# Input forms of a block-product MLP: odd tiles used where they lie, the residual's loads moved, fewer steps of a task queue

## The chip, the core and the metric

The kernel runs on one core of one Trainium2 chip. The metric is the device time of one execution in microseconds (us). Inputs and output lie in device memory (HBM); five engines work in parallel on tiles in the on-chip memory: PE multiplies matrices, DVE, ACT and POOL compute on vectors, and SP, ACT and POOL issue DMA transfers.

## The reference, cut to what matters

The reference is one decoder block in float32 for 512 tokens, D = 2048 and a hidden width of 8192. Attention, a gated recurrence and their projections come first and are not touched. The change lies in the MLP at the end:

```python
h2 = rms_norm(x, norm2_w[l]) * (1.0 + scale2) + shift2
ff = jnp.square(jax.nn.relu(h2.astype(dt) @ w_ff1[l])) @ w_ff2[l]
x = x + (gate2 * ff.astype(jnp.float32)).astype(dt)
```

`h2` is the normalised input of the title, `x` in the last line the residual.

## The kernel before, in words

**Numbers.** Every float32 operand of PE is split into a high part (a cast, on ACT) and a low part (the value minus the high part, on DVE), and each product is three matmuls: high by high, high by low, low by high. So `whi`, `vhi` are high parts of weights, `wlo`, `vlo` low ones, and a pair `hi`, `lo` of 128x512 tiles is one 128-channel slice of `h2`, transposed, for all 512 tokens. There are 16 such channel tiles, even and odd ones; all stay on chip in the pool `hp`.

**Plain stage.** The first four of the 16 hidden groups of 512 columns are computed directly (`hidden`, `first_hidden`; matmuls at L205 to L207, weight casts at L39, subtractions at L40). Meanwhile a queue of small tasks (`tasks`; one `tick()` advances it by one `yield`) prepares the **input forms**: `input_forms(u)`, u = 0 to 3, copies four channel tiles into `fs` (L1047, ACT) and `make_forms` turns them into seven block combinations by four subtractions or additions (L1017 to L1020), splits each into high and low (L1025, L1026) through staging tiles `part`, and stores them to HBM (L1028, issued by POOL): `h_hid`, `h_lod`. The same helper stores the forms of the hidden activations, `f_hid` and `f_lod`.

**Block products.** The other six pairs of hidden groups, and the whole second matrix, are computed as 2x2 block matrices with seven products instead of eight, numbered 1 to 7 and run in `order`. The first matrix has six blocks of 1024 columns; the second has two halves of the columns, q = 0 and 1, with four steps c = 0 to 3 each, which add up. One `product` consists of four steps u, and each step needs 12 matmuls (L1157 to L1159) with one `vhi` (cast at L1143) and one `vlo` (L1144). Some products first combine raw weight tiles (L1127, DVE). There is one tile each of `vhi` and `vlo` for each u: the cast for step u of the next product can start when PE is done with step u of the present one. Four raw weight tiles stand in each of four pools; SP loads the next one (L1119, 512 KB) when the last user of the old one is done. POOL loads the operands: four loads of 512 KB for a product, `Fh` and `Fl` (L1095), into four buffers each, two products ahead. Products 4 and 2 of the first matrix use the tiles `R` instead, four loads of 1 MB, loaded once and kept in the pool `res`.

**Around it.** After the first product 5 of a block, and of q = 0, c = 0, `turned` transposes the finished hidden columns and starts their forms. `residual_in(q)` issues nine loads on ACT's own queue, `gate` (L1270) and eight tiles `d` of the residual (L1274, 256 KB each); they are needed at c = 3. It is called at the end of c = 0 and placed behind the last copy `a` (L1318). The tile framework's scheduler sets the order of the instructions of each engine.

**Semaphores of transfers.** Transfers of SP and ACT together take eight completion semaphores in turn, called DMAHW0 to DMAHW7 in the listings below; those of POOL take DMASW0 to DMASW7. An issue waits until the transfer that had its semaphore before has landed. An engine issues in order, so an issue that waits on ACT holds up the casts behind it.

Of the kernel before, what the change touches and what calls it, by code (L numbers as in the profile page):

```python
# [8 lines left out]
F32 = mybir.dt.float32  # L9
# [35 lines left out]
def hybrid_block(ctx, tc, x, c, positions, norm1_w, w_ada, b_ada, w_in, q_norm_w, k_norm_w,  # L45
# [176 lines left out]
    ph = ctx.enter_context(ExitStack())  # L222
# [7 lines left out]

    def pair(i):

        return [hp.tile([P, S], F32R, name=f"{c}{i}", tag=f"{c}{i}") for c in ("hi", "lo")]
# [5 lines left out]
    for i in range(NK):  # L239
        pair(i)  # L240
    hhi, hlo, spare = [], [], []

# [762 lines left out]
    PLAIN = 4  # L1005
    KG = 4

    def forms_in_dram(name, n):
        return [dr.tile([n * FORMS * P, 512], F32, name=f"{name}_{c}d").rearrange("(g i p) n -> g i p n", i=FORMS, p=P)
                for c in ("hi", "lo")]  # L1010

    fparts, hparts = forms_in_dram("f", NG), forms_in_dram("h", KG)

    def make_forms(fs, dst, g, stage, in_place=False):

        a21, a11, a22, a12, s1, s2, s4 = (fs[:, i] for i in range(FORMS))
        dve.tensor_tensor(s1, a21, a22, op=ALU.add)  # L1017
        dve.tensor_tensor(a21, a11, a21, op=ALU.subtract)
        dve.tensor_tensor(s2, s1, a11, op=ALU.subtract)
        dve.tensor_tensor(s4, a12, s2, op=ALU.subtract)  # L1020
        yield
        for a, b in ((0, 2), (2, 4), (4, 6), (6, 7)):
            hi = stage()[:, 0:b - a]
            lo = fs[:, a:b].bitcast(F32R) if in_place else stage()[:, 0:b - a]
            act.copy(hi, fs[:, a:b])  # L1025
            dve.tensor_tensor(lo, fs[:, a:b], hi.bitcast(F32), op=ALU.subtract)  # L1026
            for d, t in zip(dst, (hi, lo)):
                pool.dma_start(d[g, a:b].rearrange("i p n -> p i n"), t.rearrange("p i a t -> p i (a t)").bitcast(F32))  # L1028
            yield

    def block(fs, j):
# [7 lines left out]
        return stg.tile([P, FORMS, 2, 256], F32, name="fs", bufs=1)  # L1039

    def plain_stage():
        return stg.tile([P, 2, 2, 256], F32R, name="part", bufs=7)

    def input_forms(u):
        fs = plain_forms()
        for j in range(4):
            act.copy(block(fs, j), halves(uT[4 * u + j]))  # L1047
# [19 lines left out]

    st_.close()
    pw.close()
    ph.close()  # L1070

    s_ = {}
    pools = {}
    for n, b in (("raw12", 4), ("spl3", 1), ("s15", 1), ("raw22", 4), ("spl1", 1), ("spl2", 1), ("s67", 1), ("raw21", 4),
                 ("fs2", 1), ("stA", 3), ("raw11", 4), ("spl0", 1), ("stB", 1), ("fp", 4)):
        pools[n] = ctx.enter_context(tc.tile_pool(name=n, bufs=b, reuse_waits="tile"))
        if n[0:2] in ("s1", "s6"):
            for i in n[1:3]:
# [12 lines left out]
    def operand(src, c, i):

        def load(t, d, g):
            n = t.shape[1]
            pool.dma_start(t.rearrange("p g a t -> p g (a t)").bitcast(F32),  # L1095
                           d[g:g + n, slot_of[i]].rearrange("g p n -> p g n"))
# [12 lines left out]

    def weights(view, g0, c0, order):  # L1110
# [8 lines left out]
                    nc.sync.dma_start(raw, view[:, g0 + u, e, :, c0 + n * 512:c0 + (n + 1) * 512])  # L1119
# [9 lines left out]
    def part(i, u, w, first):  # L1129

        b11, b12, b21, b22 = (w[u, e, n] for e in range(2) for n in range(2))
        if i == 5:
            sum_of(b11, b12, b11, first)
        if i == 6:
            sum_of(b11, b22, b11, first)
        if i == 7:
            sum_of(b12, b22, b12, first)
        if i == 4:
            sum_of(b11, b11, b21, first)
        src = {1: b11, 5: b11, 6: b11, 4: b11, 7: b12, 2: b21, 3: b22}[i]  # L1140
        hi = pools[f"spl{u}"].tile([P, 2, 512], F32R, name="vhi")
        lo = pools[f"spl{u}"].tile([P, 2, 512], F32R, name="vlo")
        act.copy(hi, src)  # L1143
        split_done.append(dve.tensor_tensor(lo, src, hi.bitcast(F32), op=ALU.subtract))  # L1144
        return hi, lo

    def product(i, src, c, w, tag, by_tile, first, early):

        banks = [bank("f2", tag=tag) for _ in range(2)]
        fh, fl = operand(src, c, i)  # L1150

        def mm(u, whi, wlo, ts_):
            for a in range(2):
                for t in ts_:
                    ts = slice(t * P, (t + 1) * P)
                    first, end = u + a == 0, u + a == KG
                    pe.matmul(banks[t], lhsT=fh[u][:, a, ts], rhs=whi[:, a], start=first, stop=False)  # L1157
                    pe.matmul(banks[t], lhsT=fh[u][:, a, ts], rhs=wlo[:, a], start=False, stop=False)  # L1158
                    pe.matmul(banks[t], lhsT=fl[u][:, a, ts], rhs=whi[:, a], start=False, stop=end)  # L1159
# [167 lines left out]

# [50 lines left out]
```

## Time and profile before

| | before |
|---|---|
| time, median of 3 runs (lowest to highest) | 2330.82 us (2326.27 to 2336.61) |
| the profiled execution: its time / its span | 2319.27 us / 2317.5 us |
| PE busy in the span | 2234.7 us (96%) |
| DVE / ACT / POOL busy | 1826.0 / 1094.9 / 457.6 us |
| mean granted PE clock | 0.991 |
| bytes moved | 606.71 MB |

The span is the time from the first to the last instruction of the profiled execution. "Busy" of an engine is the sum of its instructions' times; PE's matmuls overlap, so a busy PE can still stand at half its clock. The plain stage with its input forms runs from about 1060 to 1200 us of the span, the first matrix's block products until about 1700, the second matrix to the end: q = 0 starts c = 1 at about 1780 and c = 2 at about 1855, q = 1 at about 2085 and 2160.

### The profile page before, as it was taken

The numbers are of one execution on the slowest core, as the hardware profiler recorded it, in microseconds if no ns is written. First come the engines' busy times: TensorE is split into PE (matmuls) and PEld (weight loads), VectorE is DVE, ScalarE is ACT, GpSimd is POOL, SyncE is SP. The second block draws the span as 40 slices with busy tenths as digits, with TensorE's granted clock in tenths as the row PEclk, the third lists the DMA queues.
The fourth block names the chain that finished last, engine by engine and source line by source line (L and its number), as shares of the span: only waits on it lengthen the run. The fifth ranks groups of instructions, "written<-read, shape, count | busy, mean of one in ns | idle before, by whom it ended". The sixth has DMA issues, their size and how long they took to land.

```text
span 2317.5 us, 33148 instructions
## 1 busy us (share of the span) xinstructions
PE 2234.7 (96%) x11769; PEld 1830.5 (79%) x11769; DVE 1826.0 (79%) x2773; ACT 1094.9 (47%) x1942; POOL 457.6 (20%) x668
## 2 busy tenths in 40 slices
PE   4899999999999998999999999999998999999999
PEld 3787877887778877878887888888886888888887
DVE  6999777677876574679768988988895788967878
ACT  5555434443444552447644656555563333343332
POOL 1000022000230000001342323323232222222221
PEclk9999999999999999999999999999999999999999
DMA  9798455556554256745999799889889987999884
GB/s 327 248 339 309 130 168 159 184 168 206 173 169 159 73 188 203 231 159 181 367 379 392 253 344 355 298 301 379 312 294 365 331 281 269 362 339 330 284 300 164
DMA packets 264695, 606.71 MB, mean 262 GB/s; under 512 B 23284, under 2 KB 44032, under 8 KB 264528
## 3 DMA queue, kind: packets, MB, share of 16 engines
q1 hardware_dynamic: 186800, 332.54, 42.5%
q0 software_dynamic: 72832, 262.60, 30.9%
q10 hardware_dynamic: 4896, 9.44, 1.2%
q8 instruction: 93, 1.52, 0.3%
q14 instruction: 74, 0.61, 0.1%
HBM read 522.68 MB, written 81.81 MB: 261 GB/s over the span
## 4 chain that ended last, share of the span: by engine, by line
PE 60%; DMA 14%; DVE 13%; issue 8%; ACT 2%; POOL 2%; SPq 0%; ACTq 0%; DVEq 0%; POOLq 0%
PE f L1159 10%; PE f L1158 10%; PE f L1157 10%; DMA araw<-in_w_ada_dram 7%; PE prj L197 5%; PE prj L199 4%; PE prj L198 4%; DVE acc L129 3%; PE f L207 2%; PE f L206 2%; PE f L205 2%; DMA f_lod<-fs 2%; DMA Fl<-h_lod 2%; DVE wlo L40 2%; PE prj L206 2%
## 5 line engine op out<-in xcount | busy, mean ns | idle before, releaser
L1143 ACT CAST vhi<-raw 128x1024 fp32r<-128x1024 f32 x392 | 412.8, 1055 | 548.3 <-PE f L1159 438.6
L1144 DVE TENSOR_TENSOR vlo<-raw,vhi 128x1024 fp32r<-128x1024 f32 x392 | 476.5, 1222 | 154.7 <-ACT vhi L1143 146.8
L1157 PE MATMUL f<-vhi,Fh 128*128 128x512 f32 x1376 | 538.0, 391 | 8.7 <-DMA Fh<-h_hid 3.2
L1158 PE MATMUL f<-vlo,Fh 128*128 128x512 f32 x1376 | 538.7, 391 | 3.0 <-DVE vlo L1144 3.0
L1159 PE MATMUL f<-vhi,Fl 128*128 128x512 f32 x1376 | 537.5, 391 | 1.4 <-DMA Fl<-f_lod 1.3
L39 ACT CAST whi<-wraw 128x512 fp32r<-128x512 f32 (+1 forms) x368 | 220.1, 601 | 475.4 <-PE prj L199 343.3
L197 PE MATMUL prj<-whi,hi 128*128 128x512 f32 x896 | 367.6, 410 | 8.7 <-DVE x L921 7.4
L199 PE MATMUL prj<-whi,lo 128*128 128x512 f32 x896 | 353.4, 394 | 2.5 <-DVE lo L237 2.5
L198 PE MATMUL prj<-wlo,hi 128*128 128x512 f32 x896 | 352.4, 393 | 0.0
L40 DVE TENSOR_TENSOR wlo<-wraw,whi 128x512 fp32r<-128x512 f32 (+1 forms) x368 | 244.1, 666 | 121.5 <-ACT whi L39 118.4
L129 DVE SCALAR_TENSOR_TENSOR acc<-araw,sc,acc 128x512 f32<-128x512 f32 (+1 forms) x392 | 252.9, 672 | 97.7 <-DMA araw<-in_w_ada_dram 97.0
L1157 PEld LDWEIGHTS f<-vhi,Fh 128*128 128x128 f32 x1376 | 259.4, 189 | 63.9 <-issue 6.6
L1158 PEld LDWEIGHTS f<-vlo,Fh 128*128 128x128 f32 x1376 | 259.3, 188 | 61.8 <-DVE vlo L1144 8.3
L1159 PEld LDWEIGHTS f<-vhi,Fl 128*128 128x128 f32 x1376 | 259.3, 188 | 56.1 <-DMA Fl<-f_lod 1.8
L1127 DVE TENSOR_TENSOR raw<-raw,raw 128x1024 f32<-128x1024 f32 x224 | 268.9, 1220 | 2.5 <-DMA raw<-in_w_ff_dram 2.2
L197 PEld LDWEIGHTS prj<-whi,hi 128*128 128x128 f32 x896 | 170.2, 190 | 44.5 <-DVE x L921 8.2
L199 PEld LDWEIGHTS prj<-whi,lo 128*128 128x128 f32 x896 | 169.9, 190 | 40.8 <-DVE lo L237 3.7
L198 PEld LDWEIGHTS prj<-wlo,hi 128*128 128x128 f32 x896 | 170.7, 190 | 32.6 <-DVE wlo L40 0.4
L1095 POOL DMA_DIRECT2D Fh<-f_hid x112 | 81.1, 724 | 430.5 <-PE f L1159 415.5
L205 PE MATMUL f<-hi,whi 128*128 128x512 f32 x256 | 100.2, 391 | 0.0
L207 PE MATMUL f<-hi,wlo 128*128 128x512 f32 x256 | 99.8, 390 | 0.3 <-DVE wlo L40 0.3
L206 PE MATMUL f<-lo,whi 128*128 128x512 f32 x256 | 99.6, 389 | 0.0
(305 smaller groups left out, 2941.2 us busy)
## 6 DMA issues: line engine op xcount, KB each, us to landing
raw<-in_w_ff_dram SPq DMA_DIRECT2D x224, 512.0 KB, 10.0
araw<-in_w_ada_dram SPq DMA_DIRECT2D x384, 256.0 KB, 4.2
Fh<-f_hid POOLq DMA_DIRECT2D x112, 512.0 KB, 6.5
Fl<-f_lod POOLq DMA_DIRECT2D x112, 512.0 KB, 7.7
wraw<-in_w_in_dram SPq DMA_DIRECT2D x104, 512.0 KB, 4.0
Fh<-h_hid POOLq DMA_DIRECT2D x60, 512.0 KB, 6.8
Fl<-h_lod POOLq DMA_DIRECT2D x60, 512.0 KB, 8.3
f_hid<-part POOLq DMA_DIRECT2D x48, 512.0 KB, 7.8
```

The costliest lines, as they stand in the source:

```text
L39: nc.scalar.copy(hi, src)
L40: (eng or nc.vector).tensor_tensor(lo, src, hi.bitcast(F32), op=ALU.subtract)
L129: dve.scalar_tensor_tensor(acc, raw[:, k - k0], vec[:, k:k + 1], acc, op0=ALU.mult, op1=ALU.add)
L197: pe.matmul(banks[ti], lhsT=hi[:, ts], rhs=whi, start=first, stop=False)
L198: pe.matmul(banks[ti], lhsT=hi[:, ts], rhs=wlo, start=False, stop=False)
L199: pe.matmul(banks[ti], lhsT=lo[:, ts], rhs=whi, start=False, stop=last)
L1127: dve.tensor_tensor(dst, a, b, op=ALU.subtract)
L1143: act.copy(hi, src)
L1144: split_done.append(dve.tensor_tensor(lo, src, hi.bitcast(F32), op=ALU.subtract))
L1157: pe.matmul(banks[t], lhsT=fh[u][:, a, ts], rhs=whi[:, a], start=first, stop=False)
L1158: pe.matmul(banks[t], lhsT=fh[u][:, a, ts], rhs=wlo[:, a], start=False, stop=False)
L1159: pe.matmul(banks[t], lhsT=fl[u][:, a, ts], rhs=whi[:, a], start=False, stop=end)
```

## The change

- The pool of the 16 pairs is split: even tiles in `hp0`, which is released before the block products as before, odd ones in `hp1`, which stays until the first matrix is done. The pool `res` and its four loads `R` are gone: products 4 and 2 of the first matrix take halves of the odd pairs directly.
- `input_forms` has no copies on ACT. 32 operations of 128x256 on DVE compute four combinations from the tiles into a tile `xf`; only these four are split and stored in 16 stores of 512 KB. The block a11 needs no splitting: 16 stores of 128 KB take it from the pairs. What was stored was 14 MB and is 10 MB. `xf` takes its room from the staging tiles `part`, 7 before and 5 now.
- In `product`, `tick()` stands under a condition: as before in the first matrix, but once for each product in the second. So the last hidden forms (q = 0, c = 0) advance by one step a product.
- `residual_in(q)` is called at the end of c = 1 and placed behind the last cast of that step.

```diff
-    hp = ph.enter_context(tc.tile_pool(name="hp", bufs=1, side="right"))
+    hp1 = ph1.enter_context(tc.tile_pool(name="hp1", bufs=1, side="right"))
+    hp0 = ph0.enter_context(tc.tile_pool(name="hp0", bufs=1, side="right"))
...
+    def split_out(fs, a, b, stage, in_place, dst):
+
+        hi = stage()[:, 0:b - a]
+        lo = fs[:, a:b].bitcast(F32R) if in_place else stage()[:, 0:b - a]
+        act.copy(hi, fs[:, a:b])
+        dve.tensor_tensor(lo, fs[:, a:b], hi.bitcast(F32), op=ALU.subtract)
+        for d, t in zip(dst, (hi, lo)):
+            pool.dma_start(d.rearrange("i p n -> p i n"), t.rearrange("p i a t -> p i (a t)").bitcast(F32))
...
-        return stg.tile([P, 2, 2, 256], F32R, name="part", bufs=7)
+        return stg.tile([P, 2, 2, 256], F32R, name="part", bufs=5)
 
     def input_forms(u):
-        fs = plain_forms()
-        for j in range(4):
-            act.copy(block(fs, j), halves(uT[4 * u + j]))
-        yield
-        yield from make_forms(fs, hparts, u, plain_stage)
+
+        xf = stg.tile([P, 4, 2, 256], F32, name="xf", bufs=1)
+        s1, s2, s4, s3 = (xf[:, i] for i in range(4))
+        for a in range(2):
+            ev, od = (halves(uT[4 * u + 2 * a + e]) for e in range(2))
+            a21, a11, a22, a12 = ev[:, 0], ev[:, 1], od[:, 0], od[:, 1]
+            dve.tensor_tensor(s1[:, a], a21, a22, op=ALU.add)
+            dve.tensor_tensor(s3[:, a], a11, a21, op=ALU.subtract)
+            dve.tensor_tensor(s2[:, a], s1[:, a], a11, op=ALU.subtract)
+            dve.tensor_tensor(s4[:, a], a12, s2[:, a], op=ALU.subtract)
+            for d, t in zip(hparts, h2[4 * u + 2 * a]):
+                pool.dma_start(d[u, 1, :, a * 256:(a + 1) * 256], t[:, 256:512].bitcast(F32))
+        yield
+        for a in (0, 2):
+            split_out(xf, a, a + 2, plain_stage, False, [d[u, 4 + a:6 + a] for d in hparts])
+            yield
...
-    ph.close()
+    ph0.close()
...
         if src is hparts and i in (4, 2):
-            if i not in kept:
-                kept[i] = [load(res.tile([P, KG, 2, 256], F32R, name=f"R{n}{i}"), d, 0) for d, n in zip(src, "hl")]
-            return [[t[:, u] for u in range(KG)] for t in kept[i]]
+            half = slice(256, 512) if i == 2 else slice(0, 256)
+            return [[[h2[4 * u + 2 * a + 1][j][:, half] for a in range(2)] for u in range(KG)] for j in range(2)]
...
-                tick()
+                if u == KG - 1 or src is hparts:
+                    tick()
...
-                        done = act.copy(accs7[i, t], banks[t])
+                        act.copy(accs7[i, t], banks[t])
...
-            if c == 0:
-                with tc.issue_after(done.ins):
+            if c == 1:
+                with tc.issue_after(cast_done[-1].ins):
                     residual_in(q)
```

How the order of the instructions changes is shown at three places. The line numbers of the changed kernel differ: its operand loads are at L1119, its stores of forms at L1024, its casts of weights at L1157, `gate` at L1285 and `d` at L1289.

POOL's queue where the plain stage ends and the block products begin, before. `Fh`, `Fl` before the four `R` are the operands of the first two products (1 and 3), `f_hid` and `f_lod` the stores of the last plain group's forms, and the last row is the first operand of the third product (5):

```order
L1095 DMA Fl<-h_lod 128x2x512
L1095 DMA Rh_12602<-h_hid 128x4x512
L1095 DMA Rl_12604<-h_lod 128x4x512
L1095 DMA Rh_12705<-h_hid 128x4x512
L1095 DMA Rl_12707<-h_lod 128x4x512
L1028 DMA f_hid<-part 128x2x512 x2
L1028 DMA f_lod<-part 128x2x512
L1028 DMA f_hid<-part 128x2x512
L1028 DMA f_lod<-part 128x2x512
L1028 DMA f_hid<-part 128x512
L1028 DMA f_lod<-part 128x2x512
L1095 DMA Fh<-h_hid 128x2x512
```

The same place after; the first row again is the last operand of product 3:

```order
L1119 DMA Fl<-h_lod 128x2x512
L1024 DMA f_hid<-part 128x2x512
L1119 DMA Fh<-h_hid 128x2x512
L1024 DMA f_lod<-part 128x2x512
L1119 DMA Fl<-h_lod 128x2x512
L1024 DMA f_hid<-part 128x2x512
L1024 DMA f_lod<-part 128x2x512
L1024 DMA f_hid<-part 128x2x512
L1119 DMA Fh<-h_hid 128x2x512
```

The four `R` are gone, and product 5's first operand load stands behind one store instead of eleven issues.

ACT's queue where the residual's loads stood before, at the end of c = 0 (the casts behind them are those of c = 1):

```order
L1318 COPY a_16157<-f_16722 128x512 [waits PE_49]
L1318 COPY a_16158<-f_16723 128x512 [waits PE_49]
L1270 DMA gate_16798<-gate_453 128x1024 [waits DMASW4_49,DMASW5_49,DMASW3_49,DMASW0_49]
L1274 DMA d_16159<-x1d 128x512
L1274 DMA d_16160<-x1d 128x512
L1274 DMA d_16161<-x1d 128x512 [waits DMAHW4_49]
L1274 DMA d_16162<-x1d 128x512 [waits DMAHW5_49]
L1274 DMA d_16163<-x1d 128x512 [waits DMAHW6_49]
L1274 DMA d_16164<-x1d 128x512 [waits DMAHW7_49]
L1274 DMA d_16165<-x1d 128x512 [waits DMAHW0_49]
L1274 DMA d_16166<-x1d 128x512 [waits DMAHW1_49]
L1143 CAST vhi<-raw_16814 128x1024 [waits DVE_49]
```

ACT's queue where they stand after, at the end of c = 1, between the casts for product 2 and those for the first product of c = 2:

```order
L1157 CAST vhi<-raw_16788 128x1024 [waits DMAHW0_49,DVE_49,PE_49]
L1285 DMA gate_17338<-gate_456 128x1024 [waits DMASW7_49,DMASW4_49,DMAHW0_49,DMASW1_49,DMASW0_49]
L1289 DMA d_16119<-x1d 128x512 [waits DMAHW1_49]
L1289 DMA d_16120<-x1d 128x512 [waits DMAHW2_49]
L1289 DMA d_16121<-x1d 128x512 [waits DMAHW3_49]
L1289 DMA d_16122<-x1d 128x512 [waits DMAHW4_49]
L1289 DMA d_16123<-x1d 128x512 [waits DMAHW6_49]
L1289 DMA d_16124<-x1d 128x512 [waits DMAHW7_49]
L1289 DMA d_16125<-x1d 128x512 [waits DMAHW0_49]
L1289 DMA d_16126<-x1d 128x512 [waits DMAHW1_49]
L1157 CAST vhi<-raw_17348 128x1024 [waits DVE_49,PE_49]
```

The nine issues stand 25 casts later, still with four waits for semaphores that recent transfers hold; DMAHW6 and DMAHW7 belong to the second and third of the four weight loads that product 2's tiles make room for.

POOL's queue at the stores of the last hidden forms, in q = 0, c = 0, before:

```order
L1028 DMA f_hid<-part_16430 128x2x512
L1028 DMA f_hid<-part_16452 128x2x512
L1095 DMA Fh<-f_hid 128x2x512
L1095 DMA Fl<-f_lod 128x2x512
L1028 DMA f_lod<-fs_16353 128x2x512
L1028 DMA f_hid<-part_16474 128x2x512
L1028 DMA f_hid<-part_16508 128x512
L1028 DMA f_lod<-fs_16353 128x2x512 x2
L1028 DMA f_lod<-fs_16353 128x512
L1095 DMA Fh<-f_hid 128x2x512
```

And after:

```order
L1024 DMA f_hid<-part_16504 128x2x512
L1024 DMA f_hid<-part_16585 128x2x512
L1119 DMA Fh<-f_hid 128x2x512
L1119 DMA Fl<-f_lod 128x2x512
L1024 DMA f_lod<-fs_16313 128x2x512
L1024 DMA f_hid<-part_16670 128x2x512
L1024 DMA f_hid<-part_16751 128x512
L1024 DMA f_lod<-fs_16313 128x2x512 x2
L1024 DMA f_lod<-fs_16313 128x512
L1119 DMA Fh<-f_hid 128x2x512
```

Only the names' numbers differ: the eight stores stand between the same operand loads as before.

More of the change, by code (lines that the diff above doesn't have):

```diff
@@ L221, in hybrid_block @@
     edge.tile([P, 24], F32, name="edge_pad")
-    ph = ctx.enter_context(ExitStack())
-    hp = ph.enter_context(tc.tile_pool(name="hp", bufs=1, side="right"))
+    ph1 = ctx.enter_context(ExitStack())
+    ph0 = ctx.enter_context(ExitStack())
+    hp1 = ph1.enter_context(tc.tile_pool(name="hp1", bufs=1, side="right"))
+    hp0 = ph0.enter_context(tc.tile_pool(name="hp0", bufs=1, side="right"))
     def slot(name, dt=F32):
@@ L231, in pair @@
     def pair(i):
-        return [hp.tile([P, S], F32R, name=f"{c}{i}", tag=f"{c}{i}") for c in ("hi", "lo")]
+        return [(hp0, hp1)[i % 2].tile([P, S], F32R, name=f"{c}{i}", tag=f"{c}{i}") for c in ("hi", "lo")]
     def split_to(hl, src):
@@ L237, in split_to @@
         dve.tensor_tensor(hl[1], src, hl[0].bitcast(F32), op=ALU.subtract)
-    for i in range(NK):
+    for i in (*range(0, NK, 2), *range(1, NK, 2)):
         pair(i)
@@ L265, in hybrid_block @@
     second_scale = mod_cols(1, 1, g1c, n1c, 256, True)
-    spare.extend(hp.tile([P, 512], F32, name="araw", tag=f"{c}{k}") for k in range(8, NK) for c in ("hi", "lo"))
+    spare.extend((hp0, hp1)[k % 2].tile([P, 512], F32, name="araw", tag=f"{c}{k}")
+                 for k in range(8, NK) for c in ("hi", "lo"))
     for _ in range(8):
@@ L1006, in hybrid_block, with forms_in_dram @@
     KG = 4
-    def forms_in_dram(name, n):
-        return [dr.tile([n * FORMS * P, 512], F32, name=f"{name}_{c}d").rearrange("(g i p) n -> g i p n", i=FORMS, p=P)
+    def forms_in_dram(name, n, forms=FORMS):
+        return [dr.tile([n * forms * P, 512], F32, name=f"{name}_{c}d").rearrange("(g i p) n -> g i p n", i=forms, p=P)
                 for c in ("hi", "lo")]
-    fparts, hparts = forms_in_dram("f", NG), forms_in_dram("h", KG)
+    fparts, hparts = forms_in_dram("f", NG), forms_in_dram("h", KG, 8)
+    def split_out(fs, a, b, stage, in_place, dst):
[5 more added lines that the diff above has]
+            pool.dma_start(d.rearrange("i p n -> p i n"), t.rearrange("p i a t -> p i (a t)").bitcast(F32))
     def make_forms(fs, dst, g, stage, in_place=False):
@@ L1022, in make_forms @@
         for a, b in ((0, 2), (2, 4), (4, 6), (6, 7)):
[L1023 to L1028, printed above, removed]
+            split_out(fs, a, b, stage, in_place, [d[g, a:b] for d in dst])
             yield
@@ L1080, in hybrid_block @@
                     s_[int(i), t] = pools[n].tile([P, 512], F32, name=f"s{i}{t}")
-    res_ = ctx.enter_context(ExitStack())
-    res = res_.enter_context(tc.tile_pool(name="res", bufs=1, side="right", reuse_waits="tile"))
     slot_of = {1: 1, 2: 3, 3: 6, 4: 2, 5: 4, 6: 5, 7: 0}
+    hslot_of = {**slot_of, 7: 7}
     order = (1, 5, 6, 7, 3, 4, 2)
@@ L1105, in operand @@
             for o, d, n in zip(out_, src, "hl"):
-                t = load(pools["fp"].tile([P, 2, 2, 256], F32R, name=f"F{n}"), d, KG * c + h)
-                o.extend(t[:, u] for u in range(2))
+                t = pools["fp"].tile([P, 2, 2, 256], F32R, name=f"F{n}")
+                g = KG * c + h
+                slot_ = (hslot_of if src is hparts else slot_of)[i]
+                pool.dma_start(t.rearrange("p g a t -> p g (a t)").bitcast(F32),
+                               d[g:g + 2, slot_].rearrange("g p n -> p g n"))
+                o.extend([t[:, u, a] for a in range(2)] for u in range(2))
         return out_
@@ L1120, in weights @@
         return w
-    split_done = []
+    split_done, cast_done = [], []
     def sum_of(dst, a, b, first):
@@ L1142, in part @@
         lo = pools[f"spl{u}"].tile([P, 2, 512], F32R, name="vlo")
-        act.copy(hi, src)
+        cast_done.append(act.copy(hi, src))
         split_done.append(dve.tensor_tensor(lo, src, hi.bitcast(F32), op=ALU.subtract))
@@ L1156, in mm @@
                     first, end = u + a == 0, u + a == KG
-                    pe.matmul(banks[t], lhsT=fh[u][:, a, ts], rhs=whi[:, a], start=first, stop=False)
-                    pe.matmul(banks[t], lhsT=fh[u][:, a, ts], rhs=wlo[:, a], start=False, stop=False)
-                    pe.matmul(banks[t], lhsT=fl[u][:, a, ts], rhs=whi[:, a], start=False, stop=end)
+                    pe.matmul(banks[t], lhsT=fh[u][a][:, ts], rhs=whi[:, a], start=first, stop=False)
+                    pe.matmul(banks[t], lhsT=fh[u][a][:, ts], rhs=wlo[:, a], start=False, stop=False)
+                    pe.matmul(banks[t], lhsT=fl[u][a][:, ts], rhs=whi[:, a], start=False, stop=end)
         if by_tile:
@@ L1247, in hybrid_block @@
         tick()
-    res_.close()
+    ph1.close()
     late = ctx.enter_context(tc.tile_pool(name="late", bufs=1, side="right", reuse_waits="tile"))
```

6 lines of the change are left out of this document (removed).

## The prediction

> **What bounds the kernel now.** I read the page's shares first. PE is the bound nearly everywhere, so the change can only pay or cost where PE stands still.
>
> ```profile
> PE 2234.7 (96%) x11769; PEld 1830.5 (79%) x11769; DVE 1826.0 (79%) x2773; ACT 1094.9 (47%) x1942; POOL 457.6 (20%) x668
> ```
>
> Next the waits of PE from 1060 us to the end, the part that the change touches (total, times, longest):
>
> ```profile
> PE f L1157 <- DMA Fh<-h_hid: 3.2, 1, 3.2
> PE f L1158 <- DVE vlo L1144: 3.0, 7, 0.8
> PE f L1157 <- ACT vhi L1143: 2.8, 1, 2.8
> PE f L1157 <- DMA Fh<-f_hid: 2.7, 1, 2.7
> PE f L1159 <- DMA Fl<-f_lod: 1.3, 1, 1.3
> ```
>
> There are three stalls. The windows put them in place (busy time and count of PE, PEld, DVE, ACT, POOL; then granted clock, DMA share, GB/s):
>
> ```profile
> 1060.00:1200.00 140.00, 139.73 (x618) 115.37 (x617) 103.03 (x145) 84.97 (x139) 46.35 (x67) 1.00 0.90 330
> 1223.00:1230.20 7.20, 3.97 (x11) 2.42 (x10) 7.20 (x8) 1.05 (x1) 3.07 (x5) 0.76 1.02 397
> 1750.80:1760.00 9.20, 5.17 (x15) 3.54 (x15) 1.29 (x2) 1.05 (x2) 1.45 (x2) 0.81 1.04 392
> 1781.30:1790.30 9.00, 5.44 (x16) 3.75 (x16) 5.79 (x6) 3.94 (x5) 0.06 (x1) 0.81 0.89 332
> 1820.00:1850.00 30.00, 30.00 (x134) 24.86 (x133) 17.36 (x18) 11.61 (x11) 7.22 (x10) 1.00 1.04 387
> ```
>
> A stall costs its wait and a slow clock behind it, clock lost times window: (1 - 0.76) x 7.2 = 1.7 us at 1223, 0.19 x 9.2 = 1.7 at 1751, 0.19 x 9.0 = 1.7 at 1781. With the waits: 3.2 + 1.7 = 4.9 us (product 5's operand, the first stall), 2.7 + 1.3 + 1.7 = 5.7 (operands in c = 0, the second) and 2.8 + 0.8 + 1.7 = 5.3 (casts at the start of c = 1, the third). Everything else in these windows runs at clock 1.00 with PE full: 15.9 us are all that there is to win.
>
> **The first stall: the four R.** PE's pitch, and what it waits for:
>
> ```profile
> 1222.92 0.39 PE L1158 MATMUL f<-vlo,Fh 128*128 128x512 f32 x1
> 1223.14 0.39 PE L1159 MATMUL f<-vhi,Fl 128*128 128x512 f32 x1
> 1226.69 0.76 PE L1157 MATMUL f<-vhi,Fh 128*128 128x512 f32 x1 [3.16 <-DMA Fh<-h_hid]
> ```
>
> A matmul each 0.227 us makes 12 x 0.227 = 2.72 us for a step u and 10.9 us for a product. POOL's queue shows why that operand is late:
>
> ```profile
> 1202.07 0.75 POOL L1095 DMA_DIRECT2D Rl<-h_lod  x1 [2.31 <-PE f L207]
> 1207.36 0.71 POOL L1028 DMA_DIRECT2D f_hid<-part  x1 [4.54 <-ACT part L1025]
> ...
> 1217.53 0.73 POOL L1095 DMA_DIRECT2D Fh<-h_hid  x1 [1.90 <-DMA Rl<-h_lod]
> ```
>
> Product 5's `Fh` stands behind the last stores and waits until an `R` has landed whose semaphore it takes. Product 5 should start at 1223.4 and product 1 started two products before, at 1201.6; its first operand buffers come free 5.4 us into it, at 1207.0. After the change only one store is ahead, so the load goes out at about 1208.1. Loads issued there and shortly before landed in
>
> ```profile
> DMA to landing us min/median/max: 9.0/9.1/9.1
> DMA to landing us min/median/max: 8.9/11.2/12.5
> ```
>
> (`Fh` issued in 1217 to 1222, and in 1190 to 1200). So it is there at 1217 to 1221, before 1223.4; `Fl`, a store later (1209.6), at 1222 at the latest. **Taken: -4.9 us**; if stores run late, 0. The products 4 and 2 read the same number of weights from tiles on chip, so their matmuls cost what they cost: 0.
>
> **The plain stage.** From 1060 to 1200 the engines around PE do this (count, busy, mean ns, idle before and its releaser):
>
> ```profile
> L39 ACT CAST whi<-wraw 128x512 fp32r<-128x512 f32 x49 | 30.4, 620 | 37.4 <-PE f L206 35.6 <-issue 1.6 <-ACT part L1025 0.2
> L1026 DVE TENSOR_TENSOR part<-fs,part 128x1024 fp32r<-128x1024 f32 (+1 forms) x28 | 30.2, 1086 | 1.5 <-ACT part L1025 1.0 <-DMA f_lod<-part 0.3 <-DMA h_hid<-part 0.2
> L1025 ACT CAST part<-fs 128x1024 fp32r<-128x1024 f32 (+1 forms) x28 | 26.1, 944 | 7.5 <-DVE fs L1018 7.0 <-issue 0.5
> L1047 ACT COPY fs<-u 128x512 f32<-128x512 f32 x16 | 8.8, 616 | 1.7 <-DVE part L1026 1.7
> L1017 DVE TENSOR_TENSOR fs<-fs 128x512 f32<-128x512 f32 x7 | 4.8, 691 | 4.5 <-ACT fs L1047 4.5
> ```
>
> ACT loses 16 copies and 8 of 16 casts of input forms, 8.8 us + 8 x 0.94 = 7.5 us, 16.3 in all; DVE loses 8 x 1.09 = 8.7 us of subtractions and gains at most 32 x 0.69 - 16 x 0.69 = 11.0 us (a 256-wide operation is bounded above by the 512-wide one), so between -8.7 and +2.3; POOL issues 32 stores as before, 4 MB less. PE is busy for 139.73 of 140.00 us there and the weight casts wait for PE for 35.6 us, so all this lies beside PE: 0. The cover could go at the staging tiles: with 5 for 7, a cast may wait for a store. Now DVE waits 0.3 + 0.2 us for stores there. If a cast stood for a store's landing, the weight casts behind it on ACT would be late, and the 35.6 us in which they wait for PE are what they can give back first. I bound what is left by the longest wait for an operand in this trace, 3.2 us: 0 to +3, taken 0.
>
> **The last forms' stores.** The order puts the eight stores between the same loads as before, and the casts and subtractions that feed them stand where they stood. The `Fl` that PE waits for here is this one, from the chain of waits:
>
> ```profile
> 1742.59 13.34 DMA Fl<-f_lod
> ...
> 1755.96 0.80 PE f L1159
> ```
>
> Nothing in the issues before it changes, so the second stall stays: 0 (bounds -5.7 and 0).
>
> **The residual.** At the end of c = 0 of q = 0, and of q = 1, ACT did this:
>
> ```profile
> 1773.75 0.33 ACTq L1270 DMA_DIRECT2D gate<-gate  x1
> 1774.12 9.28 ACTq L1274 DMA_DIRECT2D d<-x1d  x8
> 1783.44 2.94 ACT L1143 CAST vhi<-raw 128x1024 fp32r<-128x1024 f32 x3 [9.23 <-DMA d<-x1d]
> 2084.37 4.93 ACTq L1274 DMA_DIRECT2D d<-x1d  x8
> 2089.35 2.95 ACT L1143 CAST vhi<-raw 128x1024 fp32r<-128x1024 f32 x3 [4.76 <-DMA gate<-gate]
> ```
>
> Eight issues last 9.3 and 4.9 us because they wait for earlier transfers; the casts behind them are late, in q = 0 too late for PE (third stall), in q = 1 just in time. The move takes the third stall away: **-5.3 us**. It puts the same nine issues behind the last cast of c = 1:
>
> ```profile
> 1844.64 1.05 ACT L1143 CAST vhi<-raw 128x1024 fp32r<-128x1024 f32 x1 [1.67 <-PE f L1159]
> 2149.28 1.06 ACT L1143 CAST vhi<-raw 128x1024 fp32r<-128x1024 f32 x1 [1.67 <-PE f L1159]
> ```
>
> That cast is released by PE's end of the product before, so PE needs the next product four steps on: 1844.6 + 4 x 2.72 = 1855.5 in q = 0, and 2160.2 in q = 1. ACT issues `gate` at 1845.7 and the first four `d` by 1848 (0.45 us each, between `gate`'s 0.33 and 4.93 / 8 = 0.62). The sixth `d` waits for the third of the four weight loads that SP issues there, at 1844.3 and 2148.9 (the fourth of five rows 2.72 us apart). Their landing times, at these places and, third, where the weights shared the DMA engines with the residual:
>
> ```profile
> L1119 SPq DMA_DIRECT2D raw<-in_w_ff_dram x5: 368/368/368, 1836.1 to 1847.0; - x5
> DMA to landing us min/median/max: 10.0/10.0/10.2
> L1119 SPq DMA_DIRECT2D raw<-in_w_ff_dram x5: 367/368/368, 2140.7 to 2151.6; - x5
> DMA to landing us min/median/max: 7.8/7.8/8.9
> L1119 SPq DMA_DIRECT2D raw<-in_w_ff_dram x2: 368/368/368, 1762.3 to 1765.6; - x2
> DMA to landing us min/median/max: 15.4/16.2/17.0
> ```
>
> After the sixth come two more issues and the cast, 3 x 0.45 + 1.05 = 2.4 us. Lower ends: 1844.3 + 10.0 + 2.4 = 1856.7, a wait of 1.2 + 0.8 for `vlo` = 2.0; in q = 1, 2148.9 + 8.9 + 2.4 = 2160.2, only the 0.8. Upper ends with 17.0: 1863.7 and 2168.3, so 8.2 + 0.8 + 1.7 = 10.7 and 8.1 + 0.8 + 1.7 = 10.6. The DMA engines are full there (1.04, 387 GB/s) and the residual adds 2 MB, so the load will be later than 10.0; but it is two thirds through when the residual starts, so earlier than 17.0. I take the middle, 13.5 and, as much later than its own row, 12.4: 1860.2 and 2163.7, waits of 4.7 and 3.5, with 0.8 and the slow clock 1.7 each **+7.2 and +6.0 us**. The eighth `d` waits for the first one's landing; at the old place the eight took
>
> ```profile
> DMA to landing us min/median/max: 7.8/11.5/13.1
> ```
>
> so from 1846.5 this ends at 1854 to 1860, within the same bounds.
>
> [...]
>
> **The sum.** -4.9 - 5.3 + 7.2 + 6.0 = +3.0 us: the profiled execution's 2319.3 becomes 2322.3. That execution is 11.5 us (0.5%) under the median of the three runs, 2330.8; on the median's scale the forecast is 2334. Its own range by the residual's ends and the first stall is -4.9 - 5.3 + 2.8 = -7.4 to 0 - 5.3 + 21.3 = +16, 2323 to 2347, but not both upper ends with the first stall left, so 2323 to 2342.
>
> **Rivals.**
> - The residual hides in its new place: the loads land as in their rows and casts catch up. Then -4.9 - 5.3 + 0 to 2.8, 2321 to 2323. For it: q = 1 hid 4.9 us of issues before without a stall of PE. Against it: ACT has 1855.5 - 1845.7 - 1.05 = 8.7 us of room there, and the wait to 1854.3 + 1.35 alone takes 9.9. Chance 0.18.
> - Slower: the residual as a third queue delays operand loads, too, beyond what two products ahead covers. A load goes out when PE has used half a product and is needed one and a half products later, 16.3 us; `Fl` in the second stall took 13.3 and was also issued late. From landings of 16.3 us on PE waits; priced as the second stall, 5.7 us in each q, +3.0 + 11.4 = 2345. Against it: at the old place the same loads made PE wait for no operand. Chance 0.09.
> - The first stall stays (stores held up by the five staging tiles, or `Fl` behind them), or the plain stage stalls by 3: +3.0 + 4.9 = 2339. For it: `part` casts released the first store at 1207.4 only. Chance 0.10.
> - The last stores spread after all, as the change's words say, and the second stall goes: +3.0 - 5.7, 2328. The order speaks against it. Chance 0.05.
>
> **How the numbers follow.** The forecast has 0.58, the rivals the rest. Half a per cent, 11.7 us, is about what a measurement of this kernel can tell from no change; it parts the cases at 2319 and 2342.5. Only the first rival at its best, with luck in the second stall too, comes under 2319: 0.08. Over 2342.5 lie the slower rival and the upper ends: 0.11. Within: 0.81. The range reaches from the first rival, 2321, to the slower one's edge, 2345.
>
> **What would show it.** Right: no wait of PE at 1223 and none at 1784; ACT's eight `d` as one group of 10 to 14 us behind the last cast of c = 1 in both q, then three casts in a row, and a wait of PE for `vhi` of 3 to 5 us at about 1845 and 2157 (1855.5 less the two gone stalls, and 2160.2 less these and with the first new one), with a clock near 0.8 in those windows; the waits for `Fh` and `Fl` in c = 0 as before. Wrong: no wait there (the weight load landed within 10 us), a wait for an operand behind the residual, or weight casts in the plain stage that wait for something other than PE.

## The result and the profile after

The changed kernel is slower by about half a per cent: 2338.26 us (median of 20 runs, 2329.06 to 2343.9) against 2323.31 us (20 runs, 2317.06 to 2336.61), a ratio of 1.0055 with a 95% interval of 1.0042 to 1.0068, or +13 us. The forecast of +3 us had the sign and the range (2321 to 2345), but the size is that of its upper end. Its 2334 us lies nearer to 2338 than its change does, and that is luck: it stood on a median of 3 runs, 2330.8, where 20 runs of the same kernel give 2323.3. Counted from 2330.8 the range reaches from -10 to +14 us. The profiled execution took 2340.68 us, its span is 2338.7 us.

The waits of PE from 1060 us on, in the profile after (total, times, longest):

```profile
PE f L1172 <- DVE vlo L1158: 9.9, 12, 4.1
PE f L1171 <- ACT vhi L1157: 6.6, 2, 5.5
PE f L1171 <- DMA Fh<-f_hid: 2.8, 1, 2.8
PE f L1173 <- DMA Fl<-f_lod: 1.2, 1, 1.2
PE f L207 <- DVE wlo L40: 0.3, 1, 0.3
```

The wait for `Fh<-h_hid` at product 5 is gone. The two operand waits of c = 0 are as before. The waits for `vhi` and `vlo` have grown, and their places are seen in the windows around the four stalls that are left (columns as before: engines' busy time, then clock, DMA share, GB/s):

```profile
1262.00:1282.00 20.00, 14.87 (x52) 11.37 (x52) 14.42 (x17) 5.04 (x5) 1.41 (x2) 0.83 0.98 350
1761.00:1774.00 13.00, 8.99 (x27) 6.56 (x26) 3.40 (x3) 2.09 (x2) 1.67 (x3) 0.74 1.04 392
1861.00:1888.00 27.00, 24.34 (x99) 19.09 (x98) 24.73 (x24) 10.78 (x11) 5.65 (x8) 0.94 0.75 270
2171.00:2202.00 31.00, 24.50 (x97) 19.11 (x96) 24.65 (x24) 10.69 (x11) 5.65 (x8) 0.89 0.65 232
```

The third and fourth are the forecast ones, at the start of c = 2 in both q. The first stands in product 4 of the first block, where the kernel before had no gap:

```profile
1255.00:1275.00 20.00, 20.00 (x98) 16.82 (x97) 18.08 (x21) 8.99 (x11) 2.89 (x4) 1.00 1.04 386
```

Waits and lost clock, as the prediction priced them:

| stall | before | after | difference | forecast |
|---|---|---|---|---|
| product 5, first block | 4.9 | 0 | -4.9 | -4.9 |
| product 4, first block | 0 | 5.1 + 0.17 x 20 = 8.5 | +8.5 | 0 |
| operands, q = 0, c = 0 | 5.7 | 4.0 + 0.26 x 13 = 7.4 | +1.7 | 0 |
| start of c = 1, q = 0 | 5.3 | 0 | -5.3 | -5.3 |
| start of c = 2, q = 0 | 0 | 2.6 + 0.06 x 27 = 4.2 | +4.2 | +7.2 |
| start of c = 2, q = 1 | 0 | 6.5 + 0.11 x 31 = 9.9 | +9.9 | +6.0 |
| sum | | | +14.1 | +3.0 |

The spans differ by more, 21.2 us, since single executions differ by some us in the attention part ahead of all this. It can be cut off at the one short wait in the plain stage, which every profile has:

```profile
1062.72 0.50 PE L207 MATMUL f<-hi,wlo 128*128 128x512 f32 x1 [0.27 <-DVE wlo L40]
```

```profile
1070.14 0.50 PE L207 MATMUL f<-hi,wlo 128*128 128x512 f32 x1 [0.28 <-DVE wlo L40]
```

(before, then after; the matmul ahead of them starts at 1062.06 and 1069.48.) From there to the end are 1255.4 and 1269.2 us, +13.8, which is the table's sum and the measured ratio. In the twelve profiles of this case that stretch starts anywhere from 1059.9 to 1071.7, with or without the odd tiles, so I put the difference ahead of it down to single executions. The table of the experiments gives the rest of the span ("from the plain stage") beside the ratio.

**The stall in product 4.** DVE in the changed kernel (`raw` is product 4's combination of weights, `s` the sum of product 7's result, `vlo` product 4's low weights):

```profile
1256.99 2.41 DVE L1141 TENSOR_TENSOR raw<-raw,raw 128x1024 f32<-128x1024 f32 x2 [1.26 <-DMA raw<-in_w_ff_dram]
1263.62 0.69 DVE L1219 TENSOR_TENSOR s<-s,f 128x512 f32<-128x512 f32 x1 [4.22 <-PE f L1173]
1264.23 1.22 DVE L1158 TENSOR_TENSOR vlo<-raw,vhi 128x1024 fp32r<-128x1024 f32 x1
...
1267.69 1.22 DVE L1141 TENSOR_TENSOR raw<-raw,raw 128x1024 f32<-128x1024 f32 x1
...
1270.63 1.22 DVE L1141 TENSOR_TENSOR raw<-raw,raw 128x1024 f32<-128x1024 f32 x1
1271.77 1.23 DVE L1158 TENSOR_TENSOR vlo<-raw,vhi 128x1024 fp32r<-128x1024 f32 x1
```

DVE stands 4.2 us, waiting for the end of product 7, with product 4's first `vlo` and two of its combinations queued behind. PE then starts product 4 and waits twice for a `vlo`, 1.0 and 4.1 us. In the kernel before, all four combinations and the first three `vlo` of product 4 stood ahead of that sum (L1204), and DVE had no wait in front of it:

```profile
1254.33 1.23 DVE L1127 TENSOR_TENSOR raw<-raw,raw 128x1024 f32<-128x1024 f32 x1 [0.78 <-DMA raw<-in_w_ff_dram]
1255.47 1.22 DVE L1144 TENSOR_TENSOR vlo<-raw,vhi 128x1024 fp32r<-128x1024 f32 x1
1256.61 1.22 DVE L1127 TENSOR_TENSOR raw<-raw,raw 128x1024 f32<-128x1024 f32 x1
1257.74 3.49 DVE L1144 TENSOR_TENSOR vlo<-raw,vhi 128x1024 fp32r<-128x1024 f32 x3
1261.15 1.28 DVE L1204 TENSOR_TENSOR s<-s,f 128x512 f32<-128x512 f32 x2
```

And the weights came late. SP, in the order of the instructions, before (the four 121xx and 122xx are the first block's last weights, 128xx the second block's):

```
L1119 DMA raw_12816<-in_w_ff_dram 128x2x512
L1119 DMA raw_12196<-in_w_ff_dram 128x2x512
L1119 DMA raw_12198<-in_w_ff_dram 128x2x512
L1119 DMA raw_12200<-in_w_ff_dram 128x2x512
L1119 DMA raw_12202<-in_w_ff_dram 128x2x512
L1119 DMA raw_12802<-in_w_ff_dram 128x2x512
```

and after (`raw_12762` is the second block's):

```
L1133 DMA raw_12776<-in_w_ff_dram 128x2x512
L1133 DMA raw_12762<-in_w_ff_dram 128x2x512
L1133 DMA raw_12164<-in_w_ff_dram 128x2x512
L1133 DMA raw_12166<-in_w_ff_dram 128x2x512
L1133 DMA raw_12168<-in_w_ff_dram 128x2x512
L1133 DMA raw_12170<-in_w_ff_dram 128x2x512
```

One load has moved ahead of four. It needs the room of a tile that a `vlo` still reads, SP waits 4.0 us for that, and the four behind it wait too. Before (the five rows from `raw_12816` to `raw_12202`) and after (from `raw_12762` to `raw_12168`; `raw_12170` follows half a microsecond later):

```profile
L1119 SPq DMA_DIRECT2D raw<-in_w_ff_dram x5: 368/650/2996, 1234.1 to 1236.8; - x5
L1133 SPq DMA_DIRECT2D raw<-in_w_ff_dram x4: 367/414/462, 1248.1 to 1249.7; - x4
```

Less the 7.4 us by which this execution is late in the plain stage, the four loads go out about 6 us later, and PE comes 4.9 us earlier.

### The profile page after: what moved, and what is told of

Same layout as the page of the kernel before. It is cut to its first block, busy times and chain, and to the rows that moved or that the text cites. A ratio compares the mean times of both kernels' runs of the same rounds, so it can differ in the third digit from the quotient of the medians.

```text
span 2338.7 us, 33097 instructions
## 1 busy us (share of the span) xinstructions
PE 2243.8 (96%) x11769; PEld 1835.9 (78%) x11769; DVE 1820.0 (78%) x2781; ACT 1080.9 (46%) x1918; POOL 446.2 (19%) x664
## 4 chain that ended last, share of the span: by engine, by line
PE 64%; DVE 16%; DMA 12%; issue 6%; ACT 2%; POOL 1%; SPq 0%; DVEq 0%; POOLq 0%; ACTq 0%
PE f L1172 9%; PE f L1173 9%; PE f L1171 9%; PE prj L197 6%; PE prj L199 6%; PE prj L198 6%; DMA araw<-in_w_ada_dram 5%; DVE vlo L1158 4%; DVE raw L1141 3%; PE f L207 2%; PE f L205 2%; PE f L206 2%; DMA Fl<-h_lod 2%; DVE acc L129 2%; PE prj L206 1%
## 5 line engine op out<-in xcount | busy, mean ns | idle before, releaser
L1157 ACT CAST vhi<-raw 128x1024 fp32r<-128x1024 f32 x392 | 412.6, 1055 | 562.3 <-PE f L1173 420.0
L1119 POOL DMA_DIRECT2D Fh<-f_hid x112 | 78.9, 705 | 443.3 <-PE f L1173 429.1
```

Of the source, the lines that this page charges most:

```text
L1157: cast_done.append(act.copy(hi, src))
```

## The experiments

Two hypotheses stood behind the numbers: ACT's late casts come from issues that wait for semaphores (and not from the residual's bytes), and the stall in product 4 comes from the two orders, SP's and DVE's (and not from the odd tiles as operands or a shortage of DVE's time). Results against runs of the kernel before on the same chip. Where the intervals of two rows overlap, the times alone don't part them, and the text goes by the stalls in the profiles:

| kernel | ratio (95% interval) | from the plain stage, us, less before's 1255.4 |
|---|---|---|
| changed kernel | 1.0055 (1.0042 to 1.0068) | +13.8 |
| e1: residual's move alone | 1.0043 (1.0028 to 1.0057) | +9.2 |
| e2: that move undone | 1.0000 (0.9988 to 1.0012) | +0.4 |
| e3: SP's order mended | 1.0044 (1.0030 to 1.0059) | +10.4 |
| e4: residual in five issues | 0.9991 (0.9980 to 1.0003) | -3.1 |
| e6: stores really apart | 1.0028 (1.0013 to 1.0042) | +7.4 |
| e8: SP's and DVE's order mended | 1.0019 (1.0003 to 1.0034) | +6.8 |
| e9: before, `R` loaded later | 1.0055 (1.0035 to 1.0074) | +11.2 |
| e10: all mends | 0.9949 (0.9931 to 0.9966) | -14.4 |
| e11: before, residual and stores mended | 0.9964 (0.9950 to 0.9978) | -9.4 |
| e12: all mends, residual at c = 0 | 0.9943 (0.9924 to 0.9962) | -15.8 |

**The residual's move alone (e1).** The kernel before with

```diff
-            if c == 0:
-                with tc.issue_after(done.ins):
+            if c == 1:
+                with tc.issue_after(cast_done[-1].ins):
                     residual_in(q)
```

> The kernel before with only the residual's loads moved to the end of c = 1. Theory (semaphores hold the casts): the stall at 1781 us goes (-5.3 us); behind the last cast of c = 1 ACT's eight d again last 10 to 15 us, because the fifth and sixth wait for weight loads issued 3 to 8 us earlier, and PE waits for vhi and vlo at the start of c = 2, 3 to 5 us with its clock in q = 0 and 7 to 11 us in q = 1. Sum +5 to +11 us against the kernel before. Rival (the new place only looks bad beside the other edits): no wait of PE for vhi there, -5 us.

Measured +10 us by the ratio, +9.2 in the profile. ACT at the end of c = 1, q = 0:

```profile
1846.51 12.24 ACTq L1274 DMA_DIRECT2D d<-x1d  x8
1858.84 3.89 ACT L1143 CAST vhi<-raw 128x1024 fp32r<-128x1024 f32 x4 [11.81 <-DMA d<-x1d]
```

PE waits there for `vhi` (3.1) and `vlo` (0.5) and loses 3.4 us of clock. In q = 1 it waits 0.7 for `vhi` and 2.8 for `vlo` with no slow clock, half or less of the 7 to 11 us expected. The move makes its own stalls without the other edits. Of the 9.2 us, some 4 are longer slow clocks and waits at the two stalls that e1 left as they were, product 5's and c = 0's (hardware, below).

**The move undone (e2).** The changed kernel with the residual's loads at the end of c = 0.

> The changed kernel with the residual's loads back at the end of c = 0. Theory: both stalls at the start of c = 2 go, the one at the start of c = 1 of q = 0 comes back (5 to 6 us); the stall in product 4 of the first block (5.1 us of waits for vlo and 3.4 us of slow clock) stays, the one of product 5's operand stays away. Sum -5 + 8.5 = about +4 us against the kernel before. Rival (the product 4 stall comes from the shifted times and not from the order): it goes too, and the sum is -5 us.

Measured 1.0000, at most 1.0012: neither the +4 us of the theory nor the -5 us of the rival. PE's waits:

```profile
PE f L1172 <- DVE vlo L1158: 8.1, 9, 4.1
PE f L1171 <- DMA Fh<-f_hid: 2.9, 1, 2.9
PE f L1171 <- ACT vhi L1157: 1.5, 1, 1.5
```

The stall at the start of c = 2 is gone in both q. Product 4 waits 5.1 us in all as in the changed kernel, with 1.7 us of slow clock instead of 3.4, so the theory was right on what stays. That of c = 1 is back at less than half its price, 1.5 + 0.8 us and no slow clock. The stalls add up to -4.9 + 6.8 - 3.0 and +1.5 at the operands of c = 0, the +0.4 of the table. So undoing the residual's move gives the whole loss back, and the product 4 stall doesn't depend on it. What the odd tiles gain at product 5 they give back at product 4.

**SP's order mended (e3).** An edge in `weights`, for the loads of the second block:

```diff
+                    late_ = tc.issue_after(held[0].ins) if len(held) == 1 and (e, n) == (0, 1) else ExitStack()
+                    with late_:
-                    nc.sync.dma_start(raw, view[...])
+                        ld = nc.sync.dma_start(raw, view[...])
+        held.append(ld)
```

> The changed kernel with one edge added on SP: the second block's load that stood before the first block's last four weight loads now stands behind them, as in the kernel before. Theory (that load waits for a subtraction on DVE and held the four loads behind it back by some 6 us): the four are issued about 6 us earlier against PE, and the waits for vlo in product 4 go, 5.1 us and the slow clock behind them, 8.5 us less than the changed kernel, about +4 us against the kernel before. Rival (operands read from the odd tiles make product 4 slow): the stall stays at 4 to 9 us, time as the changed kernel, +13 us.

Half of it came true. PE still stands 2.4 us at that place, but with no slow clock,

```profile
1262.00:1282.00 20.00, 17.57 (x84) 14.12 (x83) 16.95 (x21) 11.91 (x15) 0.10 (x1) 1.00 0.93 335
```

so the order of one load was worth some 6 of the 8.5 us there, of which 3.4 are slow clock, where e2 has 1.7 for the same stall (the whole gained 3.4, since this execution waited 3 us for casts at the start of c = 2 of q = 0, with 3.4 us of slow clock; the ratios, 1.0044 and 1.0055, don't part the two kernels). But two of product 4's combinations still stood behind DVE's wait for product 7.

**DVE's order mended too (e8).** In addition, product 7's sums are written behind product 4's subtractions:

```diff
+            if first and i == 7:
+                seventh = banks
+                continue
+            if first and i == 4:
+                with tc.issue_after(split_done[-2].ins):
+                    for t in range(2):
+                        combine(7, t, seventh[t], cs, third)
```

> The changed kernel with SP's load order mended as in the earlier run and with product 7's sums of results on DVE (first block) placed behind three of product 4's subtractions, as they stood in the kernel before. Theory (in-order DVE waits for PE's product 7 with product 4's operands queued behind it): no wait for vlo over 1 us in product 4, where 5.5 us of gaps are in the changed kernel and 2.8 with the loads alone; about +4 to +6 us against the kernel before, all of it from the residual. Rival (DVE or the loads are simply too slow there once PE comes 5 us earlier): 2 to 4 us of waits for vlo stay.

The stall is gone; the same place in this execution runs at full clock:

```profile
1250.00:1270.00 20.00, 20.00 (x98) 16.74 (x97) 17.66 (x20) 8.93 (x10) 2.83 (x4) 1.00 1.04 387
```

DVE is busy 17.7 of 20 us there and keeps up with a PE that comes 5 us earlier. So it was the order, not a shortage of DVE or of bytes; the odd tiles as operands cost PE nothing. What is left against the kernel before, +6.8 us in the profile, is the residual's two stalls (some 15 us, for the 5.3 that went) and 2.5 us more at c = 0's operands, less the 4.9 of product 5.

**The residual in five issues (e4).** The same place and bytes:

```diff
-    sums = {(r, n, t): late.tile([P, 512], F32, name=f"d{r}{n}{t}") for r in range(2) for n in range(2) for t in range(2)}
+    both = {(r, n): late.tile([P, 2, 512], F32, name=f"d{r}{n}") for r in range(2) for n in range(2)}
+    sums = {(r, n, t): d[:, t] for (r, n), d in both.items() for t in range(2)}
...
+        for (r, n), d in both.items():
+            act.dma_start(d, x1d[:, 2 - 2 * r:4 - 2 * r, q * 1024 + n * 512:q * 1024 + (n + 1) * 512])
```

> The changed kernel with the residual fetched by four loads of 512 KB instead of eight of 256 KB, at the same place: the same bytes, five issues of ACT instead of nine. Theory (the casts are held because the late issues take semaphores of transfers that have not landed): no issue waits for more than 2 us, the casts follow by about 1849 + 7 us, no wait of PE for vhi at the start of c = 2 in either q; 4.9 + 10.8 = about 15 us less than the changed kernel, -2 us against the kernel before. Rival (the residual's 2 MB delay the weights, whoever waits): PE still waits there 3 to 10 us for raw weights or casts, time about +8 to +13 us.

ACT after, in q = 0 of the changed kernel, then of e4:

```profile
1851.85 10.25 ACTq L1289 DMA_DIRECT2D d<-x1d  x8
1862.19 3.90 ACT L1157 CAST vhi<-raw 128x1024 fp32r<-128x1024 f32 x4 [9.82 <-PE f L1173]
```

```profile
1839.86 2.09 ACTq L1289 DMA_DIRECT2D d<-x1d  x4
1842.05 1.05 ACT L1157 CAST vhi<-raw 128x1024 fp32r<-128x1024 f32 x1 [1.67 <-PE f L1173]
```

Four issues take 2.1 us where eight took 10.3, the casts follow PE's pace at once, and PE has no wait there in either q. The ratio falls from 1.0055 to 0.9991, as the theory had it. The semaphores held the casts; the same bytes in fewer issues did not, though the tiles `d` took 13.8 to 23.4 us to land.

**The last stores really apart (e6).** The change's tick had left POOL's order as it was: without that condition the program's instructions stand in the same order on every engine. Here each later store stands, by an explicit edge, behind the operand loads of a later product:

```diff
         for d, t in zip(dst, (hi, lo)):
-            pool.dma_start(...)
+            with tc.issue_after(fetched[-1].ins) if apart else ExitStack():
+                pool.dma_start(...)
```

> The changed kernel with the last forms' stores placed apart for good on POOL: after the first two, each pair of stores stands behind the operand loads of a later product. Theory (the loads of c = 0 are late because up to six stores stand ahead of them in one queue): the waits for Fh and Fl there (2.8 + 1.2 us, and 3.4 us of lost clock) go, about 7 us less than the changed kernel, +6 us against the kernel before. Rival (the DMA engines are full there, so that the order of issues does not matter): waits of 3 to 6 us for operands stay in c = 0, perhaps a product later, time as the changed kernel, +13 us.

Measured 1.0028 against the changed kernel's 1.0055, and in c = 0 one wait of 0.9 us is left of 4.0, with no slow clock, although the DMA engines are as full (1.04) as before:

```profile
1752.00:1765.00 13.00, 12.08 (x54) 9.66 (x53) 5.31 (x5) 5.83 (x7) 3.98 (x6) 1.00 1.04 401
```

So the operands were late because of what stood ahead of them in POOL's queue.

**`R` later (e9).** The kernel before with its four `R` loads behind product 5's operands.

> The kernel before with one edit: the four R loads stand behind product 5's four operand loads on POOL. Theory (the 4 MB ahead made product 5's operand late): PE's wait for Fh at 1223 us goes, -3.2 us and 1.7 us of clock. What follows tells two readings apart. If the pause hid work of DVE and SP, part of it comes back as a wait for vlo or raw weights before the end of the first block, and the sum is -3 to 0 us. If the later stall came from the other edits alone, nothing follows, and the sum is -5 us.

Neither reading came true. Product 5 no longer waited over 1.3 us, but product 6 did, for 13.2 us:

```profile
PE f L1163 <- DMA Fh<-h_hid: 13.2, 1, 13.2
```

POOL shows how: the operand loads behind `R` wait, one by one, for an `R` or the load before to land.

```profile
1240.78 0.72 POOL L1099 DMA_DIRECT2D Fh<-h_hid  x1 [3.34 <-DMA Rh<-h_hid]
1244.85 0.72 POOL L1099 DMA_DIRECT2D Fl<-h_lod  x1 [3.34 <-DMA Rl<-h_lod]
```

The 4 MB hurt in both places tried in that queue, and the run says nothing on whether the old pause had hidden work; e8 does.

**All mends (e10), without the odd tiles (e11), with the old place (e12).**

> The changed kernel with all four mends: SP's load order, DVE's order in product 4, the residual by four loads of 512 KB, the last stores apart. Theory: from 1060 us on no wait of PE over 1 us is left (the small ones of 0.5 us at the blocks' starts stay); against the kernel before -4.9 - 5.3 - 5.7 = -16 us, a ratio of 0.993. Rival: the stalls only move, and half of it, -8 us, is left.

> The kernel before without the odd-tile part: only the residual by four loads of 512 KB at the end of c = 1 and the last stores apart. Theory (the odd tiles and the absence of R are worth the stall at 1223 us and nothing else): PE waits 3.2 us for Fh at product 5 of the first block and loses 1.7 to 3.4 us of clock behind it, no other wait over 1 us; -5.3 - 5.7 = -11 us against the kernel before, ratio 0.995. Rival (the odd-tile part is worth nothing, since the time comes back elsewhere in the first block): as the kernel with all mends, -13 to -14 us.

> The changed kernel with all four mends, but the residual's five issues at the end of c = 0, as before. Theory (the number of issues decides, not the place): no issue waits for a transfer that is still under way, the casts at the start of c = 1 follow in time, no wait of PE over 1 us there; as at the end of c = 1, -13 to -16 us against the kernel before. Rival (the place matters: beside the last stores the DMA engines are full, and the gate's tile must wait for the stores that now come later): PE waits 3 to 6 us for casts or operands at the start of c = 1, -6 to -10 us.

e10 is faster than the kernel before by 0.5%, 11.8 us by the ratio, which is midway between the theory's -16 and the rival's -8, and 14.4 in the profile; PE's waits from 1060 us on, e10 first, then e12:

```profile
PE f L1180 <- DVE vlo L1166: 2.3, 6, 0.4
PE f L1181 <- DMA Fl<-f_lod: 1.2, 2, 0.6
```

```profile
PE f L1180 <- DVE vlo L1166: 2.3, 6, 0.4
PE f L1181 <- DMA Fl<-f_lod: 0.3, 1, 0.3
```

No wait over 0.6 us is left in either. With five issues (e12 puts them behind the last copy of c = 0 again) the place doesn't matter: e12 is no slower. e11, which has the condition on the tick as well, keeps `R` and keeps its stall,

```profile
PE f L1160 <- DMA Fh<-h_hid: 2.8, 1, 2.8
PE f L1162 <- DMA Fl<-h_lod: 1.3, 1, 1.3
```

and is 5.0 us longer in the profile than e10. The ratios' intervals overlap (0.9950 to 0.9978 and 0.9931 to 0.9966), so the odd tiles' gain of 5 us is shown by the stall in the profiles, not by the times alone.

## Why the prediction was right, and where it was wrong

- **Product 5's operand: right.** The wait is gone in every kernel without `R`, and e11 shows it where `R` stays. Its first load went out at 1215.5, the 1208.1 of the prediction and the 7.4 us by which this execution was late. The price of 4.9 us is that of one execution: with the same stall e1 lost 7.2 us there (3.2 + 0.6 and 3.4 of clock) and e11 7.5 (2.8 + 1.3 and 3.4).
- **The plain stage at 0: right.** PE's only wait there is the same 0.3 us. The five staging tiles did make casts and subtractions wait for stores, 4.6 and 4.0 us in all, and the cover held, since the weight casts still stood 47 us for PE (after, 1067 to 1207 us):

```profile
L39 ACT CAST whi<-wraw 128x512 fp32r<-128x512 f32 x49 | 30.4, 620 | 53.6 <-PE f L206 47.2 <-issue 6.4
...
L1021 ACT CAST part<-xf 128x1024 fp32r<-128x1024 f32 x8 | 8.4, 1048 | 2.4 <-DMA h_lod<-part 1.4 <-DVE xf L1060 0.5 <-DMA f_hid<-part 0.4
```

- **"The products 4 and 2 ... cost what they cost: 0": the step that failed.** The matmuls do, as e8 shows, but the sum took the order around them as unchanged: no row of SP's or DVE's queue between products 5 and 4 stands in the prediction. SP's swapped load and DVE's order cost 8.5 us (6.8 in e2), the largest term that was missing; without it the table's sum is +5.6. The rival "the first stall stays" comes to +7.9 us, nearer to the measured change than the forecast, but by a mechanism that did not occur, since that stall went. The prediction asked what the residual's loads would meet in their new place; it did not ask what would be late next once the first stall was gone. What in the odd-tile part made the scheduler swap that load stays open. It was neither the residual's move nor the tick: e2 has the stall without the move, and e11 has the tick's condition without the odd tiles, the old order on SP and no such stall.
- **The last stores at 0: right** on the order and the waits (2.8 + 1.2 against 2.7 + 1.3). The slow clock behind them was 3.4 instead of 1.7 us.
- **The residual: mechanism right, landing times wrong, the sum right by luck.** In both q the sixth `d` did wait for the third weight load, as forecast. In q = 0 that load landed in 9.7 us, not 13.5, so 4.2 instead of 7.2. In q = 1 it landed in 14.2 us, not 12.4, with twice the slow clock behind it, so 9.9 instead of 6.0. Issue and landing of these two loads, q = 0 and q = 1:

```profile
L1133 SPq DMA_DIRECT2D raw<-in_w_ff_dram x1: 368/368/368, 1850.9 to 1850.9; - x1
DMA to landing us min/median/max: 9.7/9.7/9.7
L1133 SPq DMA_DIRECT2D raw<-in_w_ff_dram x1: 368/368/368, 2160.7 to 2160.7; - x1
DMA to landing us min/median/max: 14.2/14.2/14.2
```

  They end at 1860.6 and 2174.9, and the sixth `d` was issued then:

```profile
L1289 ACTq DMA_DIRECT2D d<-x1d x1: 325/325/325, 1860.7 to 1860.7; - x1
L1289 ACTq DMA_DIRECT2D d<-x1d x1: 327/327/327, 2174.9 to 2174.9; - x1
```

  The two errors nearly cancel: 13.2 forecast, 14.1 measured. Both parts of the forecast were off, the landing without the residual and what comes on top beside it. The rows of 10.0 and 8.9 us are the kernel before's; in this execution the weight loads issued three before these two landed in 7.4 us (q = 0) and 9.6 us (q = 1). Why they differ no run shows. The loads beside the residual took 2.3 and 4.6 us longer than these, with the first `d` issued 0.9 and 0.7 us behind them; the forecast had 3.5 us on top in both q, the middle between the rows of 10.0 and 17.0 us, which was an estimate. Nor would a load of 10.0 us issued at 1844.3 be "two thirds through" by 1848, when four `d` were to be out: 6.3 us were left.
- **The rivals.** The residual did not hide, operands behind it were not late, the first stall did not stay, and the stores did not spread.

## What to carry to other kernels

When a stall goes, the engine arrives earlier at the next in-order queue, here 4.9 us: read the order of every queue from there to the next long wait, row by row with names, since one swapped load and one sum ahead of subtractions cost 8.5 us here and gave the whole gain back. A burst of issues on an engine that also computes cost here what its semaphores' former owners still needed to land (eight issues took 10.3 and 14.7 us); the same bytes in fewer and larger transfers took the wait away (four issues, 2.1 us) where moving the burst only moved it. And a task queue that ticked less often changed nothing here, where the scheduler places the instructions: an explicit edge did (0.9 us of operand waits in c = 0, where 4.0 had been). A landing time read from one execution did not hold in the next (10.0 and 7.4 us at the same place), so a forecast that adds to one needs a range for it.

## What the runs showed of the hardware

The same stall did not cost the same slow clock. Behind the operand waits of c = 0, 4.0 us in both kernels, the clock lost 0.19 x 9.2 = 1.7 us before and 0.26 x 13 = 3.4 us after; at half clock that is 3.4 and 6.8 us of slow running. e1, which left product 5's stall as it was, lost 3.4 us there where the kernel before lost 1.7:

```profile
1226.00:1240.00 14.00, 10.25 (x31) 7.50 (x31) 13.21 (x13) 2.09 (x2) 3.62 (x6) 0.76 1.03 393
```

The clock records show the loss in these sizes. Wherever a stall from the plain stage on slowed the clock, in the profiles before and after, the granted clock is 0.50 for 3.41 or 6.83 us; behind the 13.2 us of e9 a window of 21 us had a mean clock of 0.60, a loss of 8.4 us. In the kernel before these stretches start at 1226.57, 1755.64 and 1786.36 us: 529.07 and 30.72 us apart, which is 155 and 9 times 3.413. What sets their starts and lengths no run shows. A stall that slowed the clock in these two profiles thus cost its waits and 1.7 or 3.4 us more. The length of a stall alone didn't decide: waits of 1.1 + 0.8 us (changed kernel, start of c = 2, q = 0) brought one slow stretch of 3.41 us, and waits of 1.5 + 0.8 us (e2, start of c = 1) brought none:

```profile
1786.00:1797.00 11.00, 8.70 (x37) 6.64 (x37) 7.90 (x7) 5.97 (x6) 1.77 (x3) 1.00 1.00 361
```
